# Decayed scores of an HGRN2 mixer by halved blocks instead of quartered ones

## The chip, the core and the metric

One core of a Trainium2 chip runs the whole kernel. The metric is the device time of one execution in microseconds. The kernel before takes 968.62 us (median of three runs, 966.07 to 968.62).

## The reference

The kernel computes two layers of a decoder trunk on 256 tokens of 1024 features. Each layer is a half-step SwiGLU feed-forward network (FFN), a token mixer and a second FFN, each followed by a layer norm. The mixer projects its input to five parts of 512 columns: `u` for a pooling group, and `q`, `f`, `v`, `g` for a gated linear recurrence with four heads of 128 dimensions. The recurrence is where the change lies. Within a run of tokens it is

```python
b = jnp.cumsum(g_c, axis=2)                       # g_c: log of the forget gate
rel = b[:, :, :, None, :] - b[:, :, None, :, :]
decay = jnp.exp(jnp.where(causal, rel, -jnp.inf))
scores = jnp.einsum('bhtd,bhsd,bhtsd->bhts', q_c, k_c, decay)
o_intra = jnp.einsum('bhts,bhsv->bhtv', scores, v_c)
```

The score of tokens t and s is a sum over the 128 dimensions of q, k and a decay that differs by dimension. It is no plain product of matrices, because exp(b_t) and exp(-b_s) taken alone can overflow. The output of each head is then normalised, scaled by silu(g), joined with the pooling group, and projected back by `w_out`.

## The kernel before

**Halves and streams.** The 256 tokens are two halves of 128, called `hf` 0 and 1. Every activation and weight of the large products is split into a float32r high part and a low part, and a product is three matmuls (`mm3`, L95 to L99: high by high, high by low, low by high). Weights come from memory in tiles of 128x1024 float32 through SyncE's DMA queue; ScalarE makes the high part (L102) and VectorE the low part (L103). TensorE's order is written out by hand (`manual_schedule`). The other engines' order is set by a planner, in which the weight splits have low priority.

**Slots.** Small work is put between the large matmuls by a list called `later`. Each `mm3` is one slot (`later.tick()`), and `later(n, f)` runs `f` n slots on. In the mixer, a block (`block(b, hf)`, eight slots) is one projection of one half. The order is f and q of half 0, f and q of half 1, then v, g and u of both halves. Then the two halves are multiplied by `w_out`, whose rows are taken in `WOUT_ORDER`: the recurrence's four first, then the pool's.

**Decays.** A score with a decay is split by blocks. For a block of tokens and a cut in it, with s before the cut and t after it, the decay is one factor that depends on s and one that depends on t, both at most 1. Before, blocks of 128, 32 and 8 tokens are each cut in quarters, and pairs of neighbours (blocks of 2) come by themselves. `decays` (L622 to L652) gets the logs of these factors of one head by matmul: the log gates are stationary (`lh` high, `ll` low, 128 tokens by 128 dimensions) and the moving operand is a constant matrix of zeros and ones, `cumM`, of 2 x 512 columns. Four matmuls per head (L632, L633) fill two PSUM banks, and ScalarE takes the exponential (L634) into the tile `E`. After each second head VectorE multiplies the factors of a pair of heads by the transposed k or q (L640), and GpSimd copies the odd columns of q (L639). The factors over the whole half go to `A256`, from which `cross` later gets the scores between the halves.

**Scores.** `grams` (L654 to L674), once per pair of heads, multiplies the two sides in float32: per head one product of 96 by 192 columns (stationary by moving), one of 128 by 192 and one of 128 by 256 (L660). ScalarE copies the large block's parts to `Pm` (L668); VectorE copies those of the small ones under a mask (L671, L674). `Pm` starts as a diagonal matrix, made by `diagonal`.

**Times in slots.** For each half, q is turned four slots after its block. From there `decays` of the four heads come at `lag`, +2, +4 and +6, `grams` of the first pair at `lag`+9 and of the second at `lag`+14, with `lag` = 7 + 4 x layer. `output` follows the block of g by five slots, and the turn of its result by eight more. The tile pool `psa` gives four PSUM banks in turn; the decays, the grams, `cross`, `output` and the last projection's accumulators all use it.

Of the kernel before, what the change touches and what calls it, by code (L numbers as in the profile page):

```python
# [74 lines left out]
def trunk(ctx: ExitStack, tc: tile.TileContext, t, out: bass.AP):  # L75
# [136 lines left out]
    cumM = cp.tile([P, 2, 1024], F32R, name="cumM")  # L212
    masks = cp.tile([P, 896], U8, name="masks")
# [11 lines left out]
    def load_consts():  # L225
        for j in range(2):
            cm = rawp.tile([P, 1024], F32, name="raw")
            late_dma(cm, t["cumM"][:, j, :])
            nc.scalar.copy(cumM[:, j, :], cm)
        st = rawp.tile([P, 896], F32, name="raw")  # L230
        late_dma(st, t["masks"])
        nc.vector.tensor_copy(masks, st)
# [280 lines left out]
    class Mixer:  # L513
        def __init__(self, l):
            self.l = l
            self.win = [[Weight(t["win"][l, b, kq], "w", NW) for kq in range(4)] for b in range(NB)]
            self.wout = {kt: Weight(t["wout"][l, kt], "w", NW) for kt in WOUT_ORDER}

# [3 lines left out]
    def mixer(l, win, wout):  # L522
# [14 lines left out]
        def mixed(hf):  # L537

            if hf:
                mt[hf] = xth[:, place[0]], xtl[:, place[0]]  # L540
            else:
                mt[hf] = [xtp.tile([P, KT, P], F32R, name=n) for n in ("mth", "mtl")]
            return mt[hf]

        def post_f(hf, ps):
            f = mp.tile([P, 512], F32, name="tA", bufs=2)
            nc.scalar.copy(f, ps)
            tmp = mp.tile([P, 512], F32, name="tB", bufs=2)
            ls = mp.tile([P, 512], F32, name="tC", bufs=2)
            log_sigmoid(ls, f, tmp)  # L550
            if l > 0:
                nc.vector.tensor_tensor(ls, ls, lm, ALU.add)
            kn[hf] = mp.tile([P, 512], F32, name="kn")
            nc.vector.tensor_tensor(f, ls, f, ALU.subtract)
# [12 lines left out]

            def go():
                kT[hf] = flip(kn[hf], "kT")
            later(13, go)  # L570
# [9 lines left out]
        def post_q(hf, ps):  # L580
# [28 lines left out]
        Es = [[None, None], [None, None]]  # L609
# [4 lines left out]
        def spans():  # L614

            for off, B in ((M128, 128), (M32, 32), (M8, 8)):
                for q in range(3):
                    w, n = (3 - q) * B // 4, P // B
                    yield B, n, q, off, n * w, slice((q + 1) * B // 4, B)
                    off += n * w  # L620

        def decays(hf, h):  # L622
            lh, ll = lf[hf]
            hp, j = h // 2, h % 2
            if j == 0:
                Es[hf][hp] = mp.tile([P, 2, ODD + 64], F32, name="E", bufs=2)
            E = Es[hf][hp]
            hs = slice(h * P, (h + 1) * P)
            for c in range(2):
                pe = psa.tile([P, 512], F32, name="acc")  # L630
                cs = slice(c * 512, c * 512 + 512)
                nc.tensor.matmul(pe, lh[:, hs], cumM[:, hf, cs], start=True, stop=False)  # L632
                nc.tensor.matmul(pe, ll[:, hs], cumM[:, hf, cs], start=False, stop=True)  # L633
                nc.scalar.activation(E[:, j, cs], pe, AF.Exp)  # L634
            if j == 0:
                return
            pairs = slice(2 * hp, 2 * hp + 2)
            k, q, far = kT[hf][:, pairs, :], qT[hf][:, pairs, :], A256[hf][:, pairs, :]
            nc.gpsimd.tensor_copy(E[:, :, ODD:], q[:, :, 1::2])  # L639
            mul = lambda dst, a, b: nc.vector.tensor_tensor(dst, a, b, ALU.mult)  # L640
            e = E[:, :, S128:M128]
            mul(e, e, k[:, :, 0:96])
            for _, n, _, off, size, ts in spans():
                e = blocked(E[:, :, off:off + size], n)
                mul(e, e, blocked(q, n)[:, :, :, ts])
            e32 = blocked(E[:, :, S32:FAR], 4)
            side = (k, q)[hf]
            mul(blocked(far, 4)[:, :, :, 24:32], e32[:, :, :, 24:32], blocked(side, 4)[:, :, :, 24:32])
            mul(blocked(far, 4)[:, :, :, 0:24], blocked(E[:, :, FAR:S128], 4), blocked(side, 4)[:, :, :, 0:24])
            mul(e32[:, :, :, 0:24], e32[:, :, :, 0:24], blocked(k, 4)[:, :, :, 0:24])  # L650
            e = E[:, :, S8:M8]
            mul(e, e, k)  # L652

        def grams(hf, hp):  # L654
            E = Es[hf][hp]
            scores = Pm[hf][:, 2 * hp:2 * hp + 2, :]
            ps = {B: psa.tile([P, 2, w], F32, name="acc") for B, w in ((128, 192), (32, 192), (8, 256))}
            for B, rows, s0, t0 in ((128, 96, S128, M128), (32, P, S32, M32), (8, P, S8, M8)):
                for j in range(2):
                    nc.tensor.matmul(ps[B][0:rows, j, :], E[:, j, s0:s0 + rows], E[:, j, t0:t0 + ps[B].shape[2]],  # L660
                                     start=True, stop=True)
            first = {128: M128, 32: M32, 8: M8}
            m = 0
            for B, n, q, off, size, ts in spans():
                src = ps[B][:, :, off - first[B]:off - first[B] + size]
                if B == 128:
                    rows = slice(32 * q, 32 * q + 32)
                    nc.scalar.copy(scores[rows, :, ts], src[rows])  # L668
                else:
                    mask = blocked(masks[:, m:m + 2 * size].rearrange("p (j c) -> p j c", j=2), n)  # L670
                    nc.vector.copy_predicated(blocked(scores, n)[:, :, :, ts], mask, blocked(src, n))  # L671
                    m += 2 * size
            mask = masks[:, m:m + 128].rearrange("p (j c) -> p j c", j=2)
            nc.vector.copy_predicated(scores[:, :, 1::2], mask, ps[8][:, :, 192:256])  # L674
# [12 lines left out]
        def post_g(hf, ps):  # L687
            sg[hf] = mp.tile([P, 512], F32, name="sg", bufs=2)
            nc.scalar.activation(sg[hf], ps, AF.Silu)
            later(5, lambda: output(hf))  # L690

        def output(hf):
# [17 lines left out]
            def go():  # L710
                mixed(hf)
# [3 lines left out]
                mh, ml = (m[:, 4:8, :] for m in mt[hf])  # L715
# [8 lines left out]
        def post_u(hf, ps):  # L724
# [29 lines left out]
            def mapped(pl):  # L754
# [3 lines left out]
                for g in range(4):  # L758
                    mh, ml = (m[:, g, :] for m in mt[hf])
# [6 lines left out]
        post_f(0, ps_f0)  # L766
        post_q(0, block(1, 0))
        post_f(1, block(0, 1))
        post_q(1, block(1, 1))
        for b, post in ((2, post_v), (3, post_g), (4, post_u)):  # L770
            for hf in range(2):
                ps = block(b, hf)
                if (b, hf) == (3, 0):
# [3 lines left out]
        for hf in range(2):  # L777
# [5 lines left out]
            for n, kt in enumerate(WOUT_ORDER):  # L783
                later.wait(lambda: kt // 4 in ready[hf])
                wh, wl = wout[kt].parts
                for c in range(2):
                    cs = slice(c * 512, c * 512 + 512)
                    mm3(accs[c], mt[hf][0][:, kt, :], mt[hf][1][:, kt, :], wh[:, cs], wl[:, cs],
                        n == 0, n == KT - 1)
# [20 lines left out]
def _constants():  # L810
    i = np.arange(P)
    s, tt = i[:, None], i[None, :]
    side = lambda q: (s > tt) & (s < (tt // q + 1) * q)
    parts, masks = {}, []
    for B in (128, 32, 8):
        q, parts[B] = B // 4, []
        for a in range(3):
            cols = i[i % B >= (a + 1) * q][None, :]
            ref = cols // B * B + (a + 1) * q
            parts[B].append((s >= ref) & (s <= cols))  # L820
            if B < 128:
                masks += 2 * [(s // B == cols // B) & (s % B // q == a)]
    masks += 2 * [s + 1 == i[None, 1::2]]
    cum = np.zeros((P, 2, 1024), np.float32)
    for hf, far in enumerate((s > tt, s <= tt)):
        last = i % 32 >= 24
        cum[:, hf] = np.concatenate([np.where(last, far, side(8)), far[:, ~last], side(32)[:, 0:96]]
                                    + parts[128] + parts[32] + [side(2)] + parts[8], axis=1)
# [6 lines left out]
def _layout(inputs):  # L835
# [6 lines left out]
    w_in = a["w_in"].reshape(DEPTH, KT // 2, 2, P, NB, 512)[:, :, :, :, [2, 1, 3, 4, 0]]  # L842
# [35 lines left out]
```

## Time and profile before

| | |
|---|---|
| median of three runs | 968.62 us |
| profiled execution | 968.72 us |
| its span on the core | 967.0 us |
| TensorE busy | 956.0 us, 4814 matmuls |
| VectorE busy | 653.5 us |
| ScalarE busy | 520.0 us |
| GpSimd busy | 27.7 us |
| moved by DMA | 180.68 MB |

The page shows one execution. PE is TensorE's matmuls, PEld its weight loads, DVE VectorE, ACT ScalarE, POOL GpSimd. In a group of instructions stand the line, the engine, the operation, output and inputs with their shapes and the count; behind the first bar the busy time in us and the mean duration of one in ns; behind the second the idle time of the engine just before them, in us, and what ended most of it. A matmul's shape is given as 128*128 (stationary) and 128x512 (moving). A view in order of time gives start and length in us and merges neighbours of one kind, so the length of `x8` is from the first start to the last end. A view by stretches gives the busy us of PE, PEld, DVE, ACT and POOL, then TensorE's granted clock, the DMA engines' share and GB/s. The mixer of layer 0 lies at about 193 to 284 us, that of layer 1 at about 670 to 761 us.

### The profile page before, as it was taken

Reading aid. Unit: us, or ns where it says so; the run is one execution under the profiler, and the core shown is the slowest. Engines: PE = TensorE matmul, PEld = TensorE weight load, DVE = VectorE, ACT = ScalarE, POOL = GpSimd, SP = SyncE. Lnnn points to the kernel's source line nnn. Section 1 sums busy time; section 2 is a strip of 40 time slices with the busy share of each in tenths; the row PEclk is TensorE's granted clock in tenths of the full one; section 3 lists DMA queues with packets and bytes.
Section 4 is the critical chain, followed back from the end, with each engine's and each line's share of the span. In section 5 each row is a group of like instructions: output and inputs, shape, how many; then the busy total and the mean of one; then the engine's idle time right before and its main releaser. Section 6 shows DMA issues by size and latency. Waiting matters only on the chain. (4 is left out here: it accounts for less than half of the span.)

```text
span 967.0 us, 13131 instructions
## 1 busy us (share of the span) xinstructions
PE 956.0 (99%) x4814; PEld 806.9 (83%) x4814; DVE 653.5 (68%) x1093; ACT 520.0 (54%) x808; POOL 27.7 (3%) x50
## 2 busy tenths in 40 slices
PE   9999999999999999999999999999999999999996
PEld 7888888888887888888888888888888888888885
DVE  6875656669679775756676565647897896665625
ACT  6766554367455656454446555433965466645420
POOL 0000000010010000000000000000001000000000
PEclk9999999999999999999999999999999999999999
DMA  8977775333436867564346766543334377766301
GB/s 282 339 257 264 253 244 175 112 109 132 154 109 215 308 218 240 191 208 168 119 162 242 236 209 215 167 153 98 129 133 155 103 266 282 228 224 205 127 1 44
DMA packets 51521, 180.68 MB, mean 187 GB/s; under 512 B 6272, under 2 KB 6528, under 8 KB 51456
## 3 DMA queue, kind: packets, MB, share of 16 engines
q1 hardware_dynamic: 51264, 179.31, 55.2%
q8 instruction: 38, 0.62, 0.2%
q0 software_dynamic: 192, 0.53, 0.2%
q14 instruction: 27, 0.22, 0.1%
HBM read 178.76 MB, written 1.05 MB: 186 GB/s over the span
## 5 line engine op out<-in xcount | busy, mean ns | idle before, releaser
L102 ACT CAST wh<-raw 128x1024 fp32r<-128x1024 f32 (+1 forms) x204 | 210.1, 1034 | 110.2 <-DMA raw<-in_gu 40.7
L103 DVE TENSOR_TENSOR wl<-raw,wh 128x1024 fp32r<-128x1024 f32 (+1 forms) x204 | 241.4, 1198 | 24.8 <-ACT wh L102 12.7
L310 PE MATMUL gu<-xt,wh 128*128 128x512 f32 x768 | 180.6, 391 | 0.0
L103 DVE TENSOR_TENSOR dl<-raw,dh 128x1024 fp32r<-128x1024 f32 x88 | 106.9, 1223 | 100.2 <-ACT dh L102 99.9
L310 PEld LDWEIGHTS gu<-xt,wh 128*128 128x128 f32 x768 | 144.1, 188 | 31.5
L102 ACT CAST dh<-raw 128x1024 fp32r<-128x1024 f32 x88 | 92.0, 1050 | 108.3 <-DMA raw<-in_dn 104.0
L96 PE MATMUL acc<-dh,hth 128*128 128x512 f32 x352 | 139.9, 397 | 0.0
L98 PE MATMUL acc<-dh,htl 128*128 128x512 f32 x352 | 138.2, 393 | 0.0
L97 PE MATMUL acc<-dl,hth 128*128 128x512 f32 x352 | 137.5, 391 | 0.2 <-DVE dl L103 0.2
L96 PE MATMUL gu<-wh,xt 128*128 128x512 f32 x336 | 135.0, 402 | 0.0
L98 PE MATMUL gu<-wh,xt 128*128 128x512 f32 x336 | 131.6, 392 | 0.0
L97 PE MATMUL gu<-wl,xt 128*128 128x512 f32 x336 | 131.3, 391 | 0.0
L310 PE MATMUL gu<-xt,wl 128*128 128x256 f32 x768 | 99.6, 282 | 0.0
L310 PEld LDWEIGHTS gu<-xt,wl 128*128 128x128 f32 x768 | 96.8, 191 | 1.9
L333 DVE TENSOR_TENSOR sil<-gu,sil 128x256 f32<-128x256 f32 x64 | 27.0, 422 | 92.0 <-ACT sil L332 92.0
L98 PEld LDWEIGHTS acc<-dh,htl 128*128 128x128 f32 x352 | 66.0, 188 | 14.8
L97 PEld LDWEIGHTS acc<-dl,hth 128*128 128x128 f32 x352 | 66.2, 188 | 13.2 <-DVE dl L103 0.8
L96 PEld LDWEIGHTS acc<-dh,hth 128*128 128x128 f32 x352 | 66.2, 188 | 12.0
L98 PEld LDWEIGHTS gu<-wh,xt 128*128 128x128 f32 x336 | 63.1, 188 | 13.6
L97 PEld LDWEIGHTS gu<-wl,xt 128*128 128x128 f32 x336 | 63.2, 188 | 12.6
L96 PEld LDWEIGHTS gu<-wh,xt 128*128 128x128 f32 x336 | 63.1, 188 | 12.4
L310 PE MATMUL gu<-xt,xh 128*128 128x512 f32 x256 | 62.4, 396 | 0.0
(157 smaller groups left out, 1026.7 us busy)
## 6 DMA issues: line engine op xcount, KB each, us to landing
raw<-in_gu SPq DMA_DIRECT2D x172, 512.0 KB, 4.3
raw<-in_dn SPq DMA_DIRECT2D x88, 512.0 KB, 4.6
raw<-in_win SPq DMA_DIRECT2D x40, 512.0 KB, 4.4
raw<-in_wout SPq DMA_DIRECT2D x16, 512.0 KB, 4.3
lng<-in_ln_g SPq DMA_DIRECT2D x6, 512.0 KB, 4.5
lnb<-in_ln_b SPq DMA_DIRECT2D x6, 512.0 KB, 5.8
raw<-in_gu SPq DMA_DIRECT2D x8, 256.0 KB, 6.3
raw<-in_cumM SPq DMA_DIRECT2D x2, 512.0 KB, 5.1
```

What stands on the lines that cost most here:

```text
L96: nc.tensor.matmul(ps, lh, wh, start=start, stop=False)
L97: nc.tensor.matmul(ps, lh, wl, start=False, stop=False)
L98: nc.tensor.matmul(ps, ll, wh, start=False, stop=stop)
L102: first = nc.scalar.copy(dst_h, src)
L103: return first, nc.vector.tensor_tensor(dst_l, src, dst_h.bitcast(F32), ALU.subtract)
L310: nc.tensor.matmul(ps[i][part][:, 2 * S - w:], weight.parts[lo][:, c:c + P], x[:, 0:w], start=kt == 0 and not lo, stop=kt == KT - 1 and lo ...
L333: nc.vector.tensor_tensor(dst, p[:, 0:S], dst, ALU.add)
```

## The change

Blocks of 128, 64, 32, 16, 8, 4 and 2 tokens are each cut in the middle. The columns of `E` per head are seven levels of 128, one for the factors over the whole half, and 64 for the products of level 2. Each column of the constant matrix now sums over tokens of one 64-token half only, except those over the whole half. The log gates are therefore laid out anew: `la` holds high and low parts of tokens 0 to 63 one below the other, `lb` those of tokens 64 to 127, so that one matmul gives what two gave; the columns over the whole half take one more matmul of 64 columns against ones. `decays` multiplies after the fourth head, for all four heads in one operation. `grams` takes two levels of four heads at a time, each product 128 stationary and 64 moving columns, into one bank. The times in slots are counted from the first block of f: decays at 15 + 5 x layer + 26 x half, first grams ten slots later, the others five slots apart. The block of u now comes ahead of that of g, `w_out` is taken in its own order, and `output` follows g by two slots (five for the second half of layer 1).

```diff
-S32, FAR, S128, M128, M32, S8, M8, ODD = 0, 128, 224, 320, 512, 704, 832, 1024
+LEVELS = (128, 64, 32, 16, 8, 4, 2)
+FAR = len(LEVELS) * P
-WOUT_ORDER = (4, 5, 6, 7, 0, 1, 2, 3)
...
-            lh = mp.tile([P, 512], F32R, name="lh", bufs=2)
-            ll = mp.tile([P, 512], F32R, name="ll", bufs=2)
-            halves(lh, ll, ls)
-            lf[hf] = (lh, ll)
+            lf[hf] = [mp.tile([P, 512], F32R, name=n, bufs=2) for n in ("la", "lb")]
+            lo, up = slice(0, 64), slice(64, P)
+            for part, here, there in zip(lf[hf], (lo, up), (up, lo)):
+                nc.scalar.copy(part[here], ls[here])
+                nc.vector.tensor_tensor(part[there], ls[here], part[here].bitcast(F32), ALU.subtract)
...
-                lag = 7 + 4 * l
-                for h in range(NH):
-                    later(lag + 2 * h, lambda h=h: decays(hf, h))
-                later(lag + 9, lambda: grams(hf, 0))
-                later(lag + 14, lambda: grams(hf, 1))
-                if hf == 1:
-                    later(lag + 17, cross)
...
+        def moving(hf, i, h):
+            B = LEVELS[i]
+            if B == 2:
+                return E[hf][:, h:h + 1, FAR + P:]
+            return blocked(E[hf][:, h:h + 1, i * P:(i + 1) * P], P // B)[:, :, :, B // 2:B]
 
         def decays(hf, h):
+            if h == 0:
+                E[hf] = mp.tile([P, NH, FAR + P + 64], F32, name="E")
             for c in range(2):
                 pe = psa.tile([P, 512], F32, name="acc")
-                nc.tensor.matmul(pe, lh[:, hs], cumM[:, hf, cs], start=True, stop=False)
-                nc.tensor.matmul(pe, ll[:, hs], cumM[:, hf, cs], start=False, stop=True)
-                nc.scalar.activation(E[:, j, cs], pe, AF.Exp)
+                far = c == hf
+                nc.tensor.matmul(pe, lf[hf][c][:, hs], cumM[:, hf, c, :], start=True, stop=not far)
+                if far:
+                    nc.tensor.matmul(pe[:, 448:512], lf[hf][1 - c][:, hs], ones, start=False, stop=True)
+                nc.scalar.activation(E[hf][:, h, 0:FAR + P].rearrange("p (i c n) -> p i c n", c=2, n=64)[:, :, c, :],
+                                     pe.rearrange("p (i n) -> p i n", n=64), AF.Exp)
+            if h < NH - 1:
                 return
...
+            mul(A256[hf], E[hf][:, :, FAR:FAR + P], (k, q)[hf])
+            for i, B in enumerate(LEVELS):
+                n = P // B
+                first, second = sides(B)
+                e = blocked(E[hf][:, :, i * P:(i + 1) * P], n)
+                mul(e[:, :, :, first], e[:, :, :, first], blocked(k, n)[:, :, :, first])
+                m = e[:, :, :, second]
+                if B == 2:
+                    m = blocked(E[hf][:, :, FAR + P:], n)
+                mul(m, e[:, :, :, second], blocked(q, n)[:, :, :, second])
+
+        def grams(hf, levels):
+            ps = psa.tile([P, 2, NH, 64], F32, name="acc")
+            for m, i in enumerate(levels):
+                for h in range(NH):
+                    nc.tensor.matmul(ps[:, m, h, :], E[hf][:, h, i * P:(i + 1) * P], moving(hf, i, h),
                                      start=True, stop=True)
+            for m, i in enumerate(levels):
+                if B >= 64:
+                    for b in range(n):
+                        nc.scalar.copy(Pm[hf][rows, :, b * B + B // 2:(b + 1) * B], ...)
                 else:
+                    nc.vector.copy_predicated(blocked(Pm[hf], n)[:, :, :, sides(B)[1]], ...)
...
-            later(5, lambda: output(hf))
+            later(2 + 3 * l * hf, lambda: output(hf))
...
+        for hf in range(2):
+            at = 15 + 5 * l + 26 * hf
+            for h in range(NH):
+                later(at + 2 * h, lambda hf=hf, h=h: decays(hf, h))
+            for n, levels in enumerate(((0, 1), (2, 3), (4, 5), (6,))):
+                later(at + 10 + 5 * n, lambda hf=hf, levels=levels: grams(hf, levels))
+        later(at + 16, cross)
...
-        for b, post in ((2, post_v), (3, post_g), (4, post_u)):
+        for b, post in ((2, post_v), (3, post_u), (4, post_g)):
```

More of the change, by code (lines that the diff above doesn't have):

```diff
@@ L211, in trunk @@
     nc.gpsimd.memset(neghalf, -0.5)
-    cumM = cp.tile([P, 2, 1024], F32R, name="cumM")
-    masks = cp.tile([P, 896], U8, name="masks")
+    cumM = cp.tile([P, 2, 2, 512], F32R, name="cumM")
+    ones = cp.tile([P, 64], F32R, name="ones")
+    masks = cp.tile([P, 5, 64], U8, name="masks")
     fix = cp.tile([P, 4, PAD], F32, name="fix")
@@ L228, in load_consts @@
             late_dma(cm, t["cumM"][:, j, :])
-            nc.scalar.copy(cumM[:, j, :], cm)
-        st = rawp.tile([P, 896], F32, name="raw")
+            nc.scalar.copy(cumM[:, j].rearrange("p c n -> p (c n)"), cm)
+        st = rawp.tile([P, 5 * 64], F32, name="raw")
         late_dma(st, t["masks"])
-        nc.vector.tensor_copy(masks, st)
+        nc.vector.tensor_copy(masks.rearrange("p i n -> p (i n)"), st)
+        nc.vector.memset(st[:, 0:64], 1.0)
+        nc.scalar.copy(ones, st[:, 0:64])
         late_dma(fix, t["fix"].to_broadcast([P, 4, PAD]))
@@ L516, in __init__ @@
             self.win = [[Weight(t["win"][l, b, kq], "w", NW) for kq in range(4)] for b in range(NB)]
-            self.wout = {kt: Weight(t["wout"][l, kt], "w", NW) for kt in WOUT_ORDER}
+            self.wout = {kt: Weight(t["wout"][l, kt], "w", NW) for kt in range(KT)}
         def run(self):
@@ L537, in mixed @@
         def mixed(hf):
[L539 to L542, printed above, removed]
+            if mt[hf] is None:
+                mt[hf] = ((xth[:, place[0]], xtl[:, place[0]]) if hf else
+                          [xtp.tile([P, KT, P], F32R, name=n) for n in ("mth", "mtl")])
             return mt[hf]
@@ L604, in diagonal, with sides @@
                 nc.vector.tensor_scalar_mul(Pm[hf][:, h, :], ident, dg[:, h:h + 1])
[L609 removed]
+        E = [None, None]
         def blocked(a, n):
             return a.rearrange("p j (n b) -> p j n b", n=n)
[L614 to L620, printed above, removed]
[L622 to L627 removed]
+        def sides(B):
+            return slice(0, B // 2), slice(B // 2, B)
+        def moving(hf, i, h):
[3 more added lines that the diff above has]
+            return blocked(E[hf][:, h:h + 1, i * P:(i + 1) * P], P // B)[:, :, :, B // 2:B]
+        def decays(hf, h):
+            if h == 0:
+                E[hf] = mp.tile([P, NH, FAR + P + 64], F32, name="E")
             hs = slice(h * P, (h + 1) * P)
@@ L649, in decays @@
[L649 to L660, printed above, removed]
-                                     start=True, stop=True)
[L662 to L668, printed above, removed]
-                else:
[L670 to L674, printed above, removed]
@@ L758, in mapped @@
                 for g in range(4):
-                    mh, ml = (m[:, g, :] for m in mt[hf])
+                    mh, ml = (m[:, g, :] for m in mixed(hf))
                     sc = pscale[:, l, g:g + 1]
@@ L782, in mixer @@
             accs = [psa.tile([P, 512], F32, name="acc") for _ in range(2)]
-            for n, kt in enumerate(WOUT_ORDER):
+            for kt in range(KT):
                 later.wait(lambda: kt // 4 in ready[hf])
@@ L812, in _constants @@
     s, tt = i[:, None], i[None, :]
[L813 to L824, printed above, removed]
-    for hf, far in enumerate((s > tt, s <= tt)):
-        last = i % 32 >= 24
-        cum[:, hf] = np.concatenate([np.where(last, far, side(8)), far[:, ~last], side(32)[:, 0:96]]
-                                    + parts[128] + parts[32] + [side(2)] + parts[8], axis=1)
+    sides, masks = [], []
+    for B in LEVELS:
+        middle = tt // B * B + B // 2
+        sides.append(np.where(tt < middle, (s > tt) & (s < middle), (s >= middle) & (s <= tt)))
+        if B <= 32:
+            masks.append(((s // B == tt // B) & (s < middle))[:, i % B >= B // 2])
+    cum = np.zeros((P, 2, 2, len(LEVELS) + 1, 64), np.float32)
+    for hf, far in enumerate((s > tt, s <= tt)):
+        for c in range(2):
+            half = slice(64 * c, 64 * c + 64)
+            for n, m in enumerate(sides + [far]):
+                cum[:, hf, c, n] = np.tile(m[half, half], (2, 1))
+    cum = cum.reshape(P, 2, 1024)
     masks = np.concatenate(masks, axis=1).astype(np.float32)
```

31 lines of the change are left out of this document (13 added, 18 removed).

## The prediction

> **What bounds the kernel now.** I read the page first, then TensorE's waits, then the busy time by stretch, then groups of instructions by form, then single stretches in order of time.
>
> ```profile
> span 967.0 us, 13131 instructions
> PE 956.0 (99%) x4814; PEld 806.9 (83%) x4814; DVE 653.5 (68%) x1093; ACT 520.0 (54%) x808; POOL 27.7 (3%) x50
> ```
>
> ```profile
> PE gu L381 <- DVE zero L378: 1.1, 1, 1.1
> PE acc L96 <- ACT wh L102: 0.9, 1, 0.9
> PE gu L186 <- DVE x L260: 0.7, 1, 0.7
> ```
>
> ```profile
> 190.00:290.00 100.00, 100.00 (x495) 84.12 (x494) 78.61 (x188) 58.34 (x95) 9.59 (x19) 1.00 0.39 130
> 690.00:800.00 110.00, 110.00 (x540) 92.34 (x539) 96.61 (x210) 69.55 (x108) 8.15 (x10) 1.00 0.52 174
> ```
>
> TensorE is busy 99% of the span, and its longest waits in the whole kernel add up to 2.7 us. In the two stretches that hold the mixers it never stops (100.00 of 100, 110.00 of 110), at a granted clock of 1.00, while VectorE is busy 79% and 88% and ScalarE 58% and 63%. So the change is worth what it adds to or takes from TensorE's own stream, plus any wait that it creates there. Work taken from VectorE, ScalarE or GpSimd counts only if it removes or creates such a wait.
>
> **TensorE, decays.** A matmul's mean duration holds its pipeline's tail; what it costs in a stream is the distance from start to start.
>
> ```profile
> 215.24 0.39 PE L632 MATMUL acc<-cumM,lh 128*128 128x512 f32 x1
> ...
> 216.16 0.39 PE L96 MATMUL gu<-wh,xt 128*128 128x512 f32 x1
> ```
>
> ```profile
> L632 PE MATMUL acc<-cumM,lh 128*128 128x512 f32 x32 | 12.6, 392 | 0.0
> L633 PE MATMUL acc<-cumM,ll 128*128 128x512 f32 x32 | 12.6, 392 | 0.0
> L660 PE MATMUL acc<-E 128*128 128x256 f32 x32 | 8.2, 379 | 0.0
> L660 PE MATMUL acc<-E 128*128 128x192 f32 x32 | 6.5, 326 | 0.0
> L660 PE MATMUL acc<-E 128*96 128x192 f32 x32 | 6.5, 324 | 0.0
> L660 PEld LDWEIGHTS acc<-E 128*128 128x128 f32 x64 | 11.1, 190 | 0.4
> L660 PEld LDWEIGHTS acc<-E 128*96 128x96 f32 x32 | 5.2, 162 | 0.9
> L696 PE MATMUL acc<-v,Pm 128*128 128x128 f32 x32 | 5.2, 275 | 0.0
> ```
>
> One head's decays are 4 matmuls of 512 columns from 215.24 to 216.16: 0.23 us each. There are 32+32 of them, 14.7 us. The change keeps 32 (hi and lo of 64 tokens share one load) = 7.4 us, and adds one of 64 columns per head, half and layer, 16 in all, each with its own 128x128 weight load. No row shows 64 columns. From above I take the shortest float32r matmul there is, 256 columns, in the second fence below: eight in 1.12 us, so (1.12-0.28)/7 = 0.12 us. From below, 64/512 of 0.23 = 0.03 us. I take 0.12, because the weight load is the same: 1.9 us. Decays: 7.4+1.9-14.7 = **-5.4 us** (-6.9 at the low end).
>
> **TensorE, grams.** These are float32, and each matmul of the program is two in the trace (96 for 48).
>
> ```profile
> 229.84 0.65 PE L660 MATMUL acc<-E 128*96 128x192 f32 x3
> ...
> 230.87 0.81 PE L660 MATMUL acc<-E 128*128 128x256 f32 x3
> ...
> 254.29 1.05 PE L696 MATMUL acc<-v,Pm 128*128 128x128 f32 x8
> ```
>
> ```profile
> 44.43 1.12 PE L310 MATMUL gu<-xt,wl 128*128 128x256 f32 x8
> ```
>
> Start to start, a half of 192 columns takes (0.65-0.326)/2 = 0.162 us, one of 256 (0.81-0.379)/2 = 0.216, one of 128 (1.05-0.275)/7 = 0.111. Now: 64 x 0.162 + 32 x 0.216 = 17.3 us. After: 7 levels x 4 heads x 2 token halves x 2 layers = 112 matmuls, 224 halves, each with 64 moving columns but the same 128x128 stationary side. What does such a half cost? Columns cost (0.216-0.162)/64 = 0.00084 us each, so by columns alone 64 would take 0.054 us; that is the lower end. The upper end is the 128-column half with the same kind of load, 0.111. I take 0.111: going from 192 to 128 columns the columns alone predict 0.108, and the trace gives 0.111, so the half already sits slightly above the column line; and loads last 190 ns for 128 columns and 162 for 96, 28 ns per 32, which is some 112 ns of streaming for 128 whatever is moved afterwards. So 224 x 0.111 = 24.9 us, **+7.6 us** (lower end 224 x 0.054 = 12.1, -5.2).
>
> The Trainium skill, "TensorE: Matmul & The Clock Gate", section "LDWEIGHTS (loading the stationary operand)", says that a load takes its column count over 1.2 GHz, 107 ns for 128 columns, however little is moved. By that rule the grams would be an estimated 24.0 us instead of 24.9. The rows agree (28 ns per 32 columns), and it is the rule that speaks against this change: halving the moving columns saves nothing below the load.
>
> TensorE's own stream: -5.4 + 7.6 = **+2.2 us**.
>
> **What lies beside it.** Per half and layer VectorE's multiplies go from 28 of 64 to 256 elements to 15 (14 of 256, one of 512), its predicated copies from 14 to 5, GpSimd's two copies vanish; splitting the logs becomes two ScalarE copies and two subtractions instead of one each, because 64 partitions take the time of their 512 elements.
>
> ```profile
> L640 DVE TENSOR_TENSOR E<-E,kT 128x256 f32<-128x256 f32 x8 | 3.3, 417 | 0.0
> L600 DVE TENSOR_TENSOR tB<-tA,kn 128x512 f32<-128x512 f32 x4 | 2.7, 685 | 0.0
> L671 DVE COPY_PREDICATED Pm<-masks,acc 128x192 f32<-128x192 uint8 x16 | 6.5, 405 | 2.7 <-ACT Pm L668 2.0
> L674 DVE COPY_PREDICATED Pm<-masks,acc 128x128 f32<-128x128 uint8 x8 | 3.6, 445 | 0.2
> ```
>
> ```profile
> L632 PE MATMUL acc<-cumM,lh x32: 390/393/397, 212.9 to 720.4; 128*128 128x512 f32 x32
> L102 ACT CAST lh<-tC x4: 616/630/643, 201.7 to 700.7; 128x512 fp32r<-128x512 f32 x4
> L103 DVE TENSOR_TENSOR ll<-tC,lh x4: 684/688/693, 202.3 to 701.6; 128x512 fp32r<-128x512 f32 x4
> ```
>
> I price all this at nothing on the path: TensorE does not wait for it now, and the extra 0.63+0.69 us of the split end near 204.3 (ll starts at 202.3 now and takes 0.69), and the first decay, at 212.9 now, comes four slots earlier after the change, near 210. Fewer copies may give the weight splits room; that is worth at most the few waits of the second fence.
>
> **The new distance.** Here a wait can arise. Before, seven slots lie between a pair's last decay and its grams (lag+2 to lag+9). After, all four heads' exponentials come first, and the first grams follow the fourth head's decay after four slots (at+6 to at+10). A slot is three matmuls, 0.69 us, so 2.76 us. In them must fit: two exponentials, the product into A256 and four products for levels 128 and 64. By the rows above, and 0.075 us of overlap between neighbours, VectorE needs 0.61 + 4 x 0.34 + 0.07 = 2.05 us. TensorE's queue is in order; behind the waiting gram stand the projections, so every late microsecond is a microsecond of the span.
>
> ```profile
> 207.22 0.60 PE L575 MATMUL gu<-ident,tA 128*128 128x128 f32 x4
> ...
> 207.89 0.39 PE L97 MATMUL gu<-wl,xt 128*128 128x512 f32 x1
> ...
> 240.76 0.39 PE L96 MATMUL gu<-wh,xt 128*128 128x512 f32 x1
> ...
> 696.32 0.39 PE L96 MATMUL gu<-wh,xt 128*128 128x512 f32 x1
> ```
>
> ```profile
> 215.56 1.56 ACT L634 ACTIVATE E<-acc 128x512 f32<-128x512 f32 x3
> ...
> 240.78 1.08 ACT L634 ACTIVATE E<-acc 128x512 f32<-128x512 f32 x2
> ...
> 698.77 0.62 ACT L634 ACTIVATE E<-acc 128x512 f32<-128x512 f32 x1
> ```
>
> ```profile
> 218.47 0.35 DVE L640 TENSOR_TENSOR E<-E,kT 128x192 f32<-128x192 f32 x1
> ...
> 240.05 2.35 DVE L103 TENSOR_TENSOR wl<-raw,wh 128x1024 fp32r<-128x1024 f32 x2
> ```
>
> Layer 0, first half: the decay issued at the slot where the fourth head now stands ended at 216.16, its exponentials at 217.12, and VectorE, busy with the second half's gate logs, began multiplying at 218.47: 2.3 us + 2.05 against 2.76, **1.6 us late**. Layer 0, second half: decay ends 240.76, exponentials 241.86: 1.1 + 2.05 = 3.15, **0.4 late**; the weight split in the way there (240.05, two) would add 0.5. Layer 1, first half: 696.32 to 699.39, a lag of 3.1; two groups of four transposes stand among the four slots, each 207.89 - 207.22 less one projection matmul of 0.23 = 0.44 us, so 3.6 us are available: 3.1 + 2.05 - 3.6 = 1.5 late, and I take **1.0**, since the first pair's fourteen products no longer stand ahead. Layer 1, second half: the pool's transposes (0.44 us) fall among the four slots and cover the 0.4: **0**. Together **+3.0 us**; ends 0 (the planner puts these products first everywhere) and 8 (a weight split of 1.2 us ahead of each).
>
> Later grams are five slots apart (3.4 us) and need 1.4 us of products: no wait. Moving g behind u changes one thing on the accumulators: with four banks in turn, the second bank of the last projection's second half is now that of its first half's first result, not that of an output. Its reader (L252, 0.69 us) has two groups of three matmuls, 1.38 us, to finish: no wait, up to 1 us if a weight split is ahead of it. It is in the upper end.
>
> Sum against the profiled execution: 968.7 + 2.2 + 3.0 = **973.9 us**. That execution stands 0.1 us above the median of 968.62.
>
> **Rivals.**
> - No late products: the four slots suffice. For it: the products of a gram are the first that VectorE gets, and VectorE has less to do. Against it: ScalarE's lag of 1 to 3 us in the rows above. Then 968.7 + 2.2 = 970.9.
> - The load does not bind (the other side). For it: no row has fewer than 128 moving columns, and loads may overlap further. Against it: the 128-column half off the column line. It decides as soon as a half takes under 0.10 us. At 0.054, TensorE changes by -5.2 - 6.9 = -12.1, and with 3 us late that gives 959.6. The skill's same page, section "Back-to-back issue gap", lists only some 25 ns for up to 64 columns, without the load.
> - Late everywhere: weight splits of 1.2 us get ahead of each first gram, and the accumulator bank is late too: 968.7 + 2.2 + 8 + 1 = 979.9. Against it: planner priorities keep splits back.
> - VectorE's relief ends waits outside the mixers (0.7 us at L186) and covers two thirds of the lateness: 968.7 + 2.2 + 1.0 - 0.7 = 971.2.
>
> **How the numbers follow.** Forecast 0.50 (own range 971.6 to 978), no late products 0.20, load does not bind 0.16, late everywhere 0.08, relief 0.06. A measurement of this kernel can tell 0.3%, 2.9 us, from no change: slower is above 971.5. Slower: 0.50 + 0.08 = 0.58; same: 0.20 + 0.06 = 0.26; faster: 0.16. The range reaches from 964 (a load that binds only partly) to 979, leaving out most of the unbound case below and the late one above.
>
> **What will show it.** Start to start of the 64-column float32 halves: near 0.111 us (a gram group of 16 takes some 1.8 us) if right, near 0.06 if the load does not bind. TensorE's count rises by 128 - 16 = 112 matmuls. Its waits must show grams waiting for VectorE's E, most in the first halves, about 3 us in sum; with none, the time is 971. The 64-column decays should stand 0.12 us before their successor. I am wrong if the mixers' stretches become shorter, or if they become longer by some other wait, such as the accumulator bank.

## The result and the profile after

The changed kernel takes 977.88 us (median of five runs, 974.44 to 978.80), the kernel before, on the same chip, 967.69 us (966.07 to 968.62): a ratio of 1.0105 [1.0091, 1.0119]. It is 10.2 us slower; 5.2 us were predicted. The profiled execution took 978.80 us.

First the head of the page and TensorE's longest waits of the changed kernel (in total us, times, longest):

```profile
span 977.0 us, 13234 instructions
PE 962.3 (98%) x4926; PEld 814.4 (83%) x4926; DVE 646.2 (66%) x1010; ACT 519.2 (53%) x802; POOL 23.8 (2%) x42
```

```profile
PE acc L653 <- DVE E L636: 3.3, 2, 2.1
PE gu L412 <- DVE hn L347: 1.5, 3, 0.8
PE gu L384 <- DVE zero L381: 1.1, 1, 1.1
```

TensorE has 112 matmuls more and still sets the time, but its longest wait is new: the grams (now L653) wait twice for VectorE's products (L636), 3.3 us in all. The two mixers by stretch (PE, PEld, DVE, ACT, POOL, granted clock, DMA share, GB/s), and three short stretches inside that of layer 1:

```profile
190.00:298.00 108.00, 106.79 (x581) 90.93 (x580) 81.34 (x152) 62.74 (x96) 9.05 (x15) 1.00 0.38 129
670.00:778.00 108.00, 105.88 (x556) 89.98 (x555) 80.98 (x156) 62.09 (x99) 6.76 (x10) 0.97 0.34 115
704.00:708.00 4.00, 1.88 (x11) 1.87 (x11) 3.96 (x11) 3.24 (x5) 0.00 (x0) 0.81 0.19 78
708.00:712.00 4.00, 4.00 (x14) 3.42 (x15) 3.95 (x12) 0.78 (x3) 0.00 (x0) 0.50 0.00 0
712.00:716.00 4.00, 4.00 (x23) 3.46 (x21) 0.00 (x0) 1.63 (x2) 0.00 (x0) 0.83 0.39 131
```

TensorE idles 1.2 us of the first mixer and 2.1 us of the second. In the second the granted clock falls as well: 0.81, 0.50, 0.83. Those 12 us gave 0.76 + 2.0 + 0.68 = 3.4 us less than a full clock. No term of the prediction had that. In order of time on TensorE:

```profile
706.16 3.33 PE L653 MATMUL acc<-E 128*128 128x64 f32 x16 [2.12 <-DVE E L636]
...
709.25 0.77 PE L96 MATMUL gu<-wh,xt 128*128 128x512 f32 x1
709.82 0.63 PE L97 MATMUL gu<-wl,xt 128*128 128x512 f32 x1
710.25 0.63 PE L98 MATMUL gu<-wh,xt 128*128 128x512 f32 x1
```

After an idle gap of 2.12 us the first group of 16 takes 3.33 us, and the projections behind it stand 0.57 and 0.43 us apart instead of the 0.23 of the quoted decays. What VectorE did in the gap:

```profile
703.15 0.69 DVE L636 TENSOR_TENSOR A<-E,kT 128x512 f32<-128x512 f32 x1
703.76 0.42 DVE L636 TENSOR_TENSOR E<-E,kT 128x256 f32<-128x256 f32 x1
704.19 0.68 DVE L570 TENSOR_TENSOR la<-tC,la 64x512 fp32r<-64x512 f32 x1
704.89 0.69 DVE L570 TENSOR_TENSOR lb<-tC,lb 64x512 fp32r<-64x512 f32 x1
705.59 0.42 DVE L636 TENSOR_TENSOR E<-E,qT 128x256 f32<-128x256 f32 x1
705.93 0.42 DVE L636 TENSOR_TENSOR E<-E,kT 128x256 f32<-128x256 f32 x1
```

Between the first and the second product for the grams stand the two subtractions of the doubled log split (L570), for the *second* half's logs: 1.40 us of work that nobody needs yet.

The stream itself, by groups of a form and in order of time:

```profile
L653 PE MATMUL acc<-E 128*128 128x64 f32 x224 | 28.3, 280 | 3.3 <-DVE E L636 3.3
L631 PE MATMUL acc<-ones,la 128*128 128x64 f32 x8 | 1.5, 193 | 0.0
```

```profile
232.13 1.89 PE L653 MATMUL acc<-E 128*128 128x64 f32 x16
...
237.34 1.00 PE L653 MATMUL acc<-E 128*128 128x64 f32 x8
...
697.67 0.40 PE L628 MATMUL acc<-cumM,la 128*128 128x512 f32 x1
697.91 0.19 PE L631 MATMUL acc<-ones,lb 128*128 128x64 f32 x1
697.94 0.48 PE L628 MATMUL acc<-cumM,lb 128*128 128x512 f32 x1
698.25 0.39 PE L96 MATMUL gu<-wh,xt 128*128 128x512 f32 x1
```

Sixteen halves against eight: (1.89 - 1.00)/8 = 0.111 us for one with 64 moving columns. One head's decays take 697.67 to 698.25, 0.58 us against 0.92.

Where the time went, by lengths from start to start (a mixer from ScalarE's copy of the first half's f to the last matmul of the mixer's last projection, which ends some 12 us after the stretch given in the section on the profile before; us):

| | mixer 0 | mixer 1 | rest of the span |
|---|---|---|---|
| before | 97.84 | 97.83 | 771.3 |
| after | 100.18 | 104.61 | 772.2 |

Mixer 0: +2.3 = 1.1 of stream + 1.2 of waiting. Mixer 1: +6.8, of which 1.1 is stream, 2.1 waiting and 3.4 the lower clock. The rest: +0.9, taken up again behind the experiments.

### The profile page after: what moved, and what is told of

It is laid out like the page before. It is cut to its first block, busy times and chain, and to the rows that moved or that the text cites. A ratio compares the mean times of both kernels' runs of the same rounds, so it can differ in the third digit from the quotient of the medians.

```text
span 977.0 us, 13234 instructions
## 1 busy us (share of the span) xinstructions
PE 962.3 (98%) x4926; PEld 814.4 (83%) x4926; DVE 646.2 (66%) x1010; ACT 519.2 (53%) x802; POOL 23.8 (2%) x42
## 5 line engine op out<-in xcount | busy, mean ns | idle before, releaser
L103 DVE TENSOR_TENSOR wl<-raw,wh 128x1024 fp32r<-128x1024 f32 (+1 forms) x204 | 241.1, 1197 | 36.7 <-ACT wh L102 18.2
```

The source lines that it names most:

```text
L103: return first, nc.vector.tensor_tensor(dst_l, src, dst_h.bitcast(F32), ALU.subtract)
```

## The experiments

The same lengths in the profiled execution of every run:

| | mixer 0 | mixer 1 | rest of the span |
|---|---|---|---|
| before, again (r_before) | 97.88 | 97.83 | 769.3 |
| after, again (r_after) | 101.77 | 104.64 | 771.4 |
| e1_later | 98.79 | 100.68 | 771.7 |
| e2_far_last | 99.57 | 100.31 | 772.8 |
| e3_fill | 100.19 | 101.43 | 774.7 |
| e4_short_load | 98.16 | 100.17 | 771.2 |
| e9_split_later | 98.71 | 99.95 | 770.6 |
| e8_both | 98.13 | 98.38 | 772.2 |
| e5_logs_alone | 96.16 | 96.12 | 769.6 |

The mixers before repeat within 0.04 us, the rest only within 2 us. So the mixers are the sharper measure.

**e1_later: the grams come later.**

```diff
-                later(at + 10 + 5 * n, lambda hf=hf, levels=levels: grams(hf, levels))
+                later(at + 13 + 4 * n, lambda hf=hf, levels=levels: grams(hf, levels))
```

> The changed kernel with its four gram groups at 13, 17, 21 and 25 slots behind the first decay instead of 10, 15, 20 and 25. Theory: the changed kernel's 10 us are 2.2 us of TensorE's own stream, 3.3 us of waits of the first grams for VectorE's products, some 3.4 us of halved TensorE clock that the wait of 2.1 us in layer 1 sets off, and about 1 us of smaller things. With 2.1 us more room both waits go to under 0.5 us in sum, the mean clock is 0.998 or more, and the time is 969.5 to 972 (ratio 1.002 to 1.0045). Rival A, the clock falls because of the many short float32 matmuls and not because of the idle time: the clock stays at 0.994 to 0.995 and the time is 973 to 975. Rival B, VectorE is simply behind, so the wait moves to the later groups, which are now closer together: waits of 2 us or more remain and the time is 975 or more.

Measured: 974.07 us (972.97 to 974.29), ratio 1.0067 [1.0052, 1.0082]; 3.8 us of the 10 are gone. No gram waits over 0.1 us. Of e1_later, a stretch that spans the old gap's end, and a wait of TensorE that is new:

```profile
708.00:712.00 4.00, 4.00 (x27) 3.63 (x26) 3.18 (x8) 1.64 (x3) 0.00 (x0) 1.00 0.18 45
```

```profile
PE gu L748 <- DVE tB L742: 1.0, 1, 1.0
```

Without the wait the clock stays at 1.00, in the same stretch where it was 0.50. But the time is 2 us above what was expected: in layer 1 the pool group's product (L748) now waits 1.0 us for VectorE, and mixer 1 is still 2.85 us longer than before, 1.1 of it stream, 1.0 that wait and 0.75 not placed.

**e2_far_last: the product for the cross scores after the grams' own.**

```diff
-            mul(A256[hf], E[hf][:, :, FAR:FAR + P], (k, q)[hf])
             for i, B in enumerate(LEVELS):
...
+            mul(A256[hf], E[hf][:, :, FAR:FAR + P], (k, q)[hf])
```

> The changed kernel, with the product into A256 (512 elements, 0.6 us on VectorE) behind the fourteen products of the levels instead of ahead of them. Theory: VectorE's order ahead of the first gram is what is late, so each of the two waits is shorter by about 0.6 us (3.3 to 2.1 us in sum). If the layer 1 wait of about 1.5 us no longer halves the clock, the time is 973 to 974 (clock 0.998); if it still does, 976.5 to 977.5 (clock 0.994). Rival: ScalarE's exponentials are late and VectorE would have had time; then the waits fall by less than 0.2 us in sum.

Measured: 975.47 us (974.44 to 975.93), ratio 1.0082 [1.0067, 1.0097]. Layer 1's first group in e2_far_last, in order of time:

```profile
702.77 1.10 PE L653 MATMUL acc<-E 128*128 128x64 f32 x8
704.94 1.10 PE L653 MATMUL acc<-E 128*128 128x64 f32 x8 [1.07 <-DVE E L636]
```

The product is worth 0.6 us of VectorE, yet the waits fell from 3.3 to 1.6 us: the first level's products now come before the log split, so the gap stands in the middle of the group and is 1.07 us long. The profiled execution has no stretch at half clock; in mixer 1 the clock's 3.4 us are back. The median lies between the two times expected, only 2.4 us better than the changed kernel: the other three executions, without a profile, ran at a mean clock of 0.996, where the kernel before has 0.997 to 0.999 in nearly all of its own, so the shorter gap may still have cost them some clock. That is argued, not shown.

**e3_fill: the same waiting, filled with work.** Matmuls whose results nobody reads stand ahead of the first half's first grams, four in layer 0 and eight in layer 1 (0.9 and 1.8 us). The time stays occupied; only the idleness goes.

```diff
+            if hf == 0 and levels[0] == 0:
+                idle = psg.tile([P, 512], F32, name="gu")
+                for _ in range(8 if l else 4):
+                    nc.tensor.matmul(idle, lf[0][0][:, 0:P], cumM[:, 0, 0, :], start=True, stop=True)
```

> The changed kernel with matmuls of no use ahead of the first grams of the first half: 4 of 512 columns (0.92 us) in layer 0, 8 (1.84 us) in layer 1, into a bank that nobody reads. They take the place of idle time and leave VectorE's lateness as it is. Theory: TensorE idles under 0.7 us in layer 1, the clock stays at 0.998 or more, and the time is 973.5 to 975.5: the halved clock's 3 us or so are gone, the wait's 3.3 us remain. Rival A (short float32 matmuls drop the clock): clock 0.994 to 0.995 and 977 to 979. Rival C (the filling matmuls delay the grams by their own time): 977 or more at a clock of 0.998.

Measured: 976.90 us (975.72 to 978.21), ratio 1.0095 [1.0078, 1.0111]. Two stretches and the waits of e3_fill:

```profile
708.00:712.00 4.00, 3.81 (x25) 3.51 (x26) 4.00 (x14) 2.51 (x6) 0.00 (x0) 1.00 0.00 0
```

```profile
12.00:15.00 3.00, 3.00 (x9) 2.37 (x8) 3.00 (x7) 2.63 (x6) 0.00 (x0) 0.55 1.05 413
```

```profile
PE acc L96 <- ACT wh L102: 2.2, 2, 1.7
PE acc L657 <- DVE E L636: 0.6, 2, 0.3
```

Mixer 0 is as long as after the change (100.19 and 100.18); mixer 1 is 3.2 us shorter at a clock of 1.00. So the idleness of the gap costs 3.2 us beside its length, through the clock. The median missed what was expected by 1.4 us: the profiled execution (978.07 us) waited 1.7 us for a weight in its first FFN, far from the edit. Behind that wait, too, the clock was halved, from 11.3 to 14.7 us (the second stretch), among projections of 512 columns and without a gram near; the first FFN's first accumulators end at 20.7 us there and at 18.2 to 19.0 us in every other profile, so some 2 us of this profile's long rest (774.7 us) come from there. Two of the four runs, at 975.72 and 975.74, lie near what was expected; whether the fourth (978.21) had that weight wait too, no trace shows.

**r_after and r_before: both kernels unchanged, profiled again.**

> The changed kernel once more, for the link of clock and time over its executions. Theory: executions with a mean clock of 0.994 to 0.995 take 976 to 979 us, those with 0.998 or more 974 to 975, because a halved clock of 6.8 us costs 3.4 us; layer 0's mixer is 2.3 us longer than before in all of them, layer 1's 3.4 or 6.8. Rival: times of 974 and of 978 come at one and the same clock; then the difference is in the FFNs' weights and not in the clock.

> The kernel before once more, for a second profile: how far its stretches (first FFN, mixers, starts of the FFNs behind them) differ from execution to execution. Theory: the two mixers repeat within 0.2 us, the FFN starts differ by up to 1 us, so that differences of that size outside the mixers say nothing of the change.

Measured: r_before 966.75 us; r_after 979.24 us (976.32 to 980.40), ratio 1.0120 [1.0098, 1.0141]. Two stretches of r_after, one in each layer:

```profile
224.00:228.00 4.00, 4.00 (x19) 3.20 (x19) 3.95 (x6) 1.24 (x3) 0.00 (x0) 0.76 0.19 50
...
708.00:712.00 4.00, 4.00 (x14) 3.49 (x14) 4.00 (x13) 0.78 (x3) 0.00 (x0) 0.50 0.00 0
```

Here layer 0's gap of 1.2 us halved the clock too, and mixer 0 is 101.77 us instead of 100.18. Over the nine executions of the changed kernel the time follows the mean granted clock: 0.999 goes with 974.44 us, 0.995 and 0.996 with 976.32 to 977.88, 0.992 to 0.994 with 978.67 to 980.40. The one execution at 0.999 (without a trace; the kernel before reaches that clock too) came 0.5 us above the 973.9 that was forecast with no loss of clock.

**e9_split_later: only the second half's log split moves.** It is the doubled split that the prediction priced at nothing.

```diff
+            def split():
                 lf[hf] = [mp.tile([P, 512], F32R, name=n, bufs=2) for n in ("la", "lb")]
...
+            if hf:
+                later(10 + 4 * l, split)
+            else:
+                split()
```

> The changed kernel with the split of the second half's log gates (two ScalarE copies of 0.62 us, two VectorE subtractions of 0.69 us) put off by 10 slots in layer 0 and 14 in layer 1, behind the products of the first half; it isn't needed before slot 41. In the changed kernel's profile both subtractions stand between the products of layer 1's first half (704.19 to 705.59), and one copy ahead of the last exponential of layer 0's. Theory: the split, doubled by the change, is part of what makes the first grams late; the wait of layer 1 falls from 2.1 to 0.8 us, that of layer 0 from 1.2 to about 0.6, the clock stays at 0.998, and the time is 972 to 974.5. Rival: the products and exponentials alone are too long for four slots; the waits fall by less than 0.5 us in sum and the time stays at 976 or more.

Measured: 971.90 us (971.08 to 974.20), ratio 1.0051 [1.0034, 1.0067]. TensorE's wait for the grams, and VectorE at the place of the gap, in e9_split_later:

```profile
PE acc L658 <- DVE E L641: 0.7, 1, 0.7
```

```profile
700.45 0.69 DVE L641 TENSOR_TENSOR A<-E,kT 128x512 f32<-128x512 f32 x1
701.05 0.42 DVE L641 TENSOR_TENSOR E<-E,kT 128x256 f32<-128x256 f32 x1
701.39 0.42 DVE L641 TENSOR_TENSOR E<-E,qT 128x256 f32<-128x256 f32 x1
```

The products run one behind the other, the waits fall from 3.3 to 0.7 us (layer 0's 1.2 us go altogether, layer 1's 2.1 become 0.7), and the clock stays full. The time lies 0.1 us under the range expected. With the grams where the change put them, 6.0 us of the 10.2 hang on when the planner lets VectorE and ScalarE split the second half's logs: 2.6 of waiting and 3.4 of clock add up to the same 6.0.

**e4_short_load: fewer stationary columns.** On top of e1_later. For blocks of 128 only the first 64 stationary columns carry scores, for blocks of 64 the first 96; the others are left out, which changes no score.

```diff
+                rows = slice(0, P - LEVELS[i] // 2 if i < 2 else P)
...
-                    nc.tensor.matmul(ps[:, m, h, :], E[hf][:, h, i * P:(i + 1) * P], moving(hf, i, h),
+                    nc.tensor.matmul(ps[rows, m, h, :], E[hf][:, h, i * P:i * P + rows.stop], moving(hf, i, h),
```

> The kernel with the later grams, and with the stationary side of level 128 cut to the first 64 columns and that of level 64 to the first 96 (the others carry no score); the 64 moving columns stay. Theory (the stationary load sets the pace, 0.875 ns per column): float32 halves start 0.056 us apart at level 128, 0.084 at level 64 and 0.112 at the others; 32 x 0.056 + 32 x 0.028 = 2.7 us less than with the later grams alone, 967 to 969.5. Rival (load and moving columns follow one another, 56 ns each at 128 and 64 columns): 0.085 and 0.098 us, 1.3 us less. Rival (a fixed cost per short matmul): 0.112 at all levels, no change.

Measured: 971.98 us (971.26 to 973.29), ratio 1.0049 [1.0034, 1.0064]. Groups of a form, and then three windows of the first group in order of time, of e4_short_load:

```profile
L654 PE MATMUL acc<-E 128*64 128x64 f32 x32 | 2.7, 227 | 0.1
L654 PE MATMUL acc<-E 128*96 128x64 f32 x32 | 3.6, 254 | 0.0
```

```profile
221.25 0.56 PE L654 MATMUL acc<-E 128*64 128x64 f32 x6
...
221.25 0.62 PE L654 MATMUL acc<-E 128*64 128x64 f32 x7
...
221.99 0.67 PE L654 MATMUL acc<-E 128*96 128x64 f32 x6
```

With the same 64 moving columns a half takes 0.62 - 0.56 = 0.06 us for 64 stationary columns, (0.67 - 0.254)/5 = 0.083 for 96, and 0.111 for 128. The load sets the pace, nearly in proportion to the stationary columns; 96 against 128 is the proof, since at 64 the prediction's line for moving columns alone (0.054 us) lies close as well. Against e1_later the profiles show 0.63 and 0.51 us less in the two mixers, the medians 2.1 us; 2.7 were expected. The change of length costs something itself: the first group took 1.34 us from its first start to that of the next product instead of some 1.71, while 8 x (0.111 - 0.06) + 8 x (0.111 - 0.083) would be 0.63 less, not 0.37.

**e8_both: all three cures of the grams at once** (e2's order, e4's short loads, grams 12, 16, 20 and 25 slots on).

```diff
-                later(at + 10 + 5 * n, lambda hf=hf, levels=levels: grams(hf, levels))
+                later(at + (12, 16, 20, 25)[n], lambda hf=hf, levels=levels: grams(hf, levels))
```

> The changed kernel with all three repairs: A256's product last, grams at 12, 16, 20 and 25 slots, short stationary sides at levels 128 and 64. Theory: no gram waits over 0.3 us, full clock; the stream is 1.5 us over that of the kernel before and the short loads take 2.3 off: 967 to 969.5 (ratio 0.999 to 1.002). Rival: what VectorE does later (the pool's sums, the FFNs' weights) is now what TensorE waits for, as with the later grams alone: 970 to 972.

Measured: 970.18 us (968.86 to 971.24, eight runs), ratio 1.0030 [1.0019, 1.0041]. The mixer of layer 1 in e8_both, and a wait outside the mixers, in e8_both and in the kernel before:

```profile
670.00:778.00 108.00, 107.93 (x586) 91.30 (x585) 87.22 (x164) 66.10 (x104) 6.77 (x10) 1.00 0.40 131
```

```profile
PE gu L412 <- DVE hn L347: 1.3, 3, 0.5
```

```profile
PE gu L409 <- DVE hn L344: 0.2, 1, 0.2
```

No gram waits over 0.1 us, the clock is full, and the mixers are within 0.3 and 0.55 us of before, where 0.8 us less than before were expected. The time is above the range expected and in that of the rival: 3.2 us over the 967.02 us of the kernel before in the same series, of which the mixers hold 0.8. The rest lies outside them: 1.3 us are a wait for VectorE's `hn`, the product in an FFN (0.2 us before), and the remainder is not placed. So the mixers with seven halved levels come back nearly to the old length, but not below it, and the kernel as a whole does not.

**e5_logs_alone: the kernel before, with the logs by half-token groups and nothing else of the change.** Blocks keep their quarters, grams and slots. Of the 1024 columns per head, the 512 over the whole half still take two matmuls; the 512 of blocks of 32, 8 and 2 tokens belong to one half of the tokens each, and take two matmuls of 256. With it go a packed constant matrix, another order of the columns and one more exponential per head.

```diff
-            for c in range(2):
...
-                nc.tensor.matmul(pe, lh[:, hs], cumM[:, hf, cs], start=True, stop=False)
-                nc.tensor.matmul(pe, ll[:, hs], cumM[:, hf, cs], start=False, stop=True)
...
+            la, lb = (part[:, hs] for part in lf[hf])
...
+            nc.tensor.matmul(pe, la, cumM[:, 0, 224 * hf:224 * hf + 512], start=True, stop=False)
+            nc.tensor.matmul(pe, lb, cumM[:, 1, 224 * hf:224 * hf + 512], start=False, stop=True)
...
+            nc.tensor.matmul(pe[:, 0:256], la, cumM[:, 0, 736:992], start=True, stop=True)
+            nc.tensor.matmul(pe[:, 256:512], lb, cumM[:, 1, 736:992], start=True, stop=True)
```

> One part of the change alone, on the kernel before: the log gates laid out as high over low of 64 tokens, with the quartered blocks, pairs of heads, grams and slots of the kernel before. The 512 columns per head of blocks of 32 and 8 tokens sum within one half of 64 tokens and need one matmul of 256 columns per half instead of two of 512; those of blocks of 128 keep two of 512. Theory: per head 0.46 + 2 x 0.12 = 0.70 us instead of 0.92, 16 heads: 3.5 us less in the stream, 963.5 to 965 (ratio 0.996 to 0.9975). What made the changed kernel slow is then its grams and their distance alone. Rival: the layout itself costs (a second ScalarE copy and VectorE subtraction, one more exponential per head) and makes the grams of layer 1 wait by 1 us or more: 965.5 to 967.5. Rival: matmuls on the new layout are no faster, 0.23 us each at 256 columns: no change.

Measured: 964.29 us (962.96 to 965.90, eight runs) against 966.90 (twelve runs), ratio 0.9973 [0.9962, 0.9983]. That is within the range expected, and faster than both kernels, by 2.6 us against the one before. One head's decays in e5_logs_alone, and the mixer of layer 1:

```profile
212.52 0.39 PE L634 MATMUL acc<-cumM,la 128*128 128x512 f32 x1
212.75 0.39 PE L635 MATMUL acc<-cumM,lb 128*128 128x512 f32 x1
212.98 0.28 PE L638 MATMUL acc<-cumM,la 128*128 128x256 f32 x1
213.10 0.28 PE L639 MATMUL acc<-cumM,lb 128*128 128x256 f32 x1
213.22 0.40 PE L97 MATMUL gu<-wh,xt 128*128 128x512 f32 x1
```

```profile
670.00:778.00 108.00, 108.00 (x540) 91.13 (x539) 93.15 (x209) 72.54 (x121) 9.14 (x13) 1.00 0.42 142
```

A head takes 0.70 us instead of 0.92; eight heads in a mixer make 1.76 us, and the mixers are 1.68 and 1.71 us shorter. The doubled log split is in this kernel too, and TensorE doesn't stop once in the mixers: seven slots between decays and grams cover it.

## Why the prediction was right or wrong

The direction was right; 973.9 us was 4 us too low, and 977.88 lies inside the range, near its upper end. That it does is luck in part: the upper end was left for late weight splits and a late accumulator bank, and neither came.

- **Decays, -5.4 us: right.** 0.92 - 0.58 = 0.34 us for each of 16 heads makes -5.4. The 64-column matmul takes 0.58 - 2 x 0.23 = 0.12 us, the end that was chosen. The sign named for it did not show: it starts only 0.03 us before its successor, and the successor takes 0.31 us instead of 0.23.
- **Grams, +7.6 us: right.** 0.111 us a half with 64 moving columns, and e4_short_load shows why: the pace goes with the stationary columns. The rival in which the load does not bind (959.6) is refuted. By the Trainium skill, "TensorE: Matmul & The Clock Gate", section "LDWEIGHTS (loading the stationary operand)", a load takes its columns over 1.2 GHz, which makes an estimated 53, 80 and 107 ns for 64, 96 and 128 columns; the runs gave 60, 83 and 111 ns a half.
- **"Together +3.0 us" of late first grams: right in sum (3.3), not in its parts.** Layer 0's first half waited 1.2 instead of 1.6 us, layer 1's 2.1 instead of 1.0, and the second halves not at all; that the sum agrees is luck. The shares had been worked out from the lag of the two exponentials and the products. The wait came from elsewhere, as the next point says.
- **"I price all this at nothing on the path" was the step that failed.** It held for the logs of the *first* half, whose decays come late enough. The *second* half's split has the same work on ScalarE and VectorE, and the planner put VectorE's part of it between the first half's products: 1.40 us of the 2.12 us gap. e9_split_later moved that split alone and took away 2.6 of the 3.3 us of waiting, all of layer 0's among them. Cover that TensorE has "now" was taken for cover after a change that shortens it from seven slots to four.
- **A mechanism was missing: an idle gap can lower the clock.** Every late microsecond was counted as one microsecond of the span. Layer 1's 2.1 us cost another 3.4. e3_fill shows it best: with the gap filled by useless matmuls, the clock stays at 1.00 and mixer 1 loses 3.2 us. The rival that fewer copies relieve VectorE has the wrong sign; "late everywhere" named weight splits and the accumulator bank, and neither waited.
- **The later grams and the accumulator bank, "no wait": right.** All waiting stands in the first groups of the first halves.

Medians differ by 10.2 us: 2.2 of stream, 3.3 of waiting and 3.4 of clock make 8.9. The last 1.3 us stay open in part. They would be outside the mixers, where the profiles of the changed order show 770.6 to 772.8 us (e3_fill, with its weight wait, 774.7), and those of the old order 771.3, 769.3 and 769.6. Some of it shows in the waits: for `hn`, in the FFNs, TensorE waits 1.5 us in the profile after (second line of its waits) and 0.3 to 1.8 in the others of the changed order, but 0.2, under 0.1 and 0.6 in the three of the old one. Why VectorE is later there, and whether the new order of blocks is the cause, was not tried.

## What to carry to other kernels

In these runs half of a float32 product with a fresh stationary side of 128 columns cost 0.111 us with 64 moving columns as with 128: there, cut stationary columns or use fewer products, since splitting into more and smaller ones only adds. When the distance between a producer and the matmul that waits for it is shortened, list everything that may run on the producing engines in that distance, also work for a later stage that a planner is free to put there. And price a gap on an otherwise full TensorE at more than its length, because the clock may fall behind it (here 3.4 us behind a gap of 2.12); a change whose parts have opposite signs (here the logs alone at -1.7 us a mixer, the grams at +3.8) is better taken apart.

## What the runs showed of the hardware

Gaps of 2.12 us, and once in two profiles one of 1.21 us, in a stream that was busy before and after, were followed by TensorE at half clock; so was e3_fill's wait of 1.66 us near the kernel's start. The stretches at half clock lasted 3.413 us (layer 0 in the second profile, and the first FFN of e3_fill) and 6.827 us (layer 1, both profiles), that is one or two times the same length; in the mixers they cost 1.6 and 3.4 us. The Trainium skill, "TensorE: Matmul & The Clock Gate", section "What's actually happening", gives a free-running window of 3413 ns, and the lengths agree. The same page of the Trainium skill, section "Why this matters for your kernels", asks for no idle gaps above about 3 us; here less than that was enough, and the measurement decides.

The same gap need not do it: layer 0's 1.21 us left the clock alone in the first profile, and so did e2_far_last's gap of 1.07 us in its one profile. One of the nine executions, without a trace, ran at a mean clock of 0.999, which leaves room for less than 3 us at half clock. How long a gap must be, and what decides between two equal ones, was not measured.
